# A hybrid decoder layer on one core: the first loads on two queues, the first projection's loop reordered, the planner's clocks and the final norm rewritten

## The chip, the cores and the metric

The kernel runs on one core of a Trainium2 chip. The metric is the device time of one execution in microseconds; lower is better. Three runs of the kernel before the change took 1147.87, 1148.01 and 1148.03 us.

Engine names as in the profile: PE is the matrix engine (PEld its weight loads), DVE the vector engine, ACT the activation engine, POOL the general engine. SP only issues transfers here; "SPq" and "ACTq" are the instruction streams on which a transfer is issued.

## The reference

Input x is 256 tokens by 2048 channels, everything in float32, one layer, then a final norm:

```python
def reference(x, norm1_w, w_in, ..., final_norm_w):
    for l in range(DEPTH):                                  # DEPTH = 1
        h = rmsnorm(x, norm1_w[l])
        x = x + token_mixer(h, w_in[l], ...)                # retention, mLSTM, S5, then w_out
        h = rmsnorm(x, norm2_w[l])
        x = x + conv_ffn(h, ffn_w_up[l], ...)               # 2048 -> 2 x 5632 -> 2048
    return rmsnorm(x, final_norm_w)

def token_mixer(h, w_in, ..., w_out):
    proj = h @ w_in
    r_q, r_k, r_v, r_g, m_qk, m_v, m_o, m_gates, s_u = jnp.split(proj, splits, axis=-1)
    ret_out = jax.nn.silu(r_g) * head_groupnorm(retention(rotary(r_q), rotary(r_k), r_v), ret_gn_w)
    mlstm_out = jax.nn.sigmoid(m_o) * head_groupnorm(mlstm(mq, mk, m_v, i_pre, f_pre), mlstm_gn_w)
    s5_out = s5(s_u, s5_A_re, s5_A_im, s5_log_step, ...)    # diagonal complex scan, gelu, GLU
    return jnp.concatenate([ret_out, mlstm_out, s5_out], axis=-1) @ w_out
```

`rmsnorm` is `x * rsqrt(mean(x*x) + eps) * w`. The S5 part needs, from parameters alone, `exp`, `cos` and `sin` of small tables (128x16 here); the kernel works them out with polynomials on DVE and POOL.

## The kernel before

**Split products.** Every weight chunk (128 rows by up to 1024 columns) is loaded in float32 into a tile `wr` (or `s`, for the first projection's pairs) by one transfer issued at L385. ACT casts it to the high part `wh` (L193), and DVE subtracts to get the low part `wl` (L183). Activations are split the same way: a 512-column tile holds the high part of 256 tokens, then the low part. PE multiplies `wh` with all 512 columns and `wl` with the high 256. The buffers are four `wr`, four `wh` and three `wl`. Nearly all of V's (DVE's) operations are recorded at L183, POOL's at L218, ACT's at L193 or L202 and PE's at L235 (L239 for one transpose helper), because helpers issue them.

**The front.** The first thing to be projected is the S5 input `u`: 16 K tiles of x (128 channels each) against 512 columns of weights `wu`. The loop `for j, ks in enumerate(kts)` runs over ten units: units 0 to 3 are one K tile each (weights 128x512, 256 KB; x 128 KB), units 4 to 9 are two K tiles each (weights 128x1024, 512 KB; x 256 KB). All 20 transfers of x and `wu` are issued by SP, x of a unit just ahead of its weights; the first parameters `pp0` come on ACT's stream. In the loop each unit casts its weights (`highs_to`), splits its x (ACT for the high part with the norm's weight as scale, DVE for the low part), subtracts its low weights (`lows_to`) and then issues eight matmuls for each K tile into four accumulators (`acc, acc, u, u`). `fill(n)` puts n of the small S5 parameter operations (`s5_exps`, 128x16 on DVE) between them; one DVE value of these is the root of a long POOL chain. `square()` squares x for the norm's sum.

**The first norm.** The sum of squares is reduced on PE by matmuls with a matrix of ones (`onesm`), DVE scales it, POOL takes the power -0.5 (`neg_half`) in the midst of its S5 chain, PE transposes that row with `ident` (L239) and the result `rbc` scales the projections.

**The middle, to about 412 us.** The order of all engines is set by a planner. It keeps a modelled clock for each engine (`clk.dve`, `clk.act`, `clk.pe`, `clk.pool`, `clk.dma`); each helper adds a modelled cost in `run()`, and `pump()` steps background generators (retention, gates, mLSTM, S5) when the modelled DVE clock allows. The modelled costs are not times of the chip; they only decide the order. S5's scans, its 128x512 products and the mLSTM's denominators (`t<-mis`, a DVE copy of 128x3 out of PSUM) are such background work.

**The end.** After 412 us a scheduler places the feed-forward part. `last_norm(h)` finishes both token halves: the last two K tiles of the output channels, the sum of squares, the power on POOL, a broadcast by PE (`bc`), the products on DVE, and nine output transfers (L1484, L1491). Each half's group 3 holds 128 columns of `t * r * nft`; for h = 1 it goes out together with channel group 6.

## Time and profile before

| | |
|---|---|
| median of three runs | 1148.01 us |
| profiled execution, its own time | 1147.89 us |
| its span | 1145.8 us |
| PE busy | 1133.7 us, 99% of the span |
| DVE busy | 867.4 us, 76% |
| ACT busy | 626.3 us, 55% |
| POOL busy | 74.8 us, 7% |
| share of the chain that ended last | PE 97%, DVE 2% |
| granted PE clock | 0.998 |
| HBM traffic | 212 MB read, 187 GB/s over the span |

The span runs from the first to the last recorded instruction; the execution's own time is 2.1 us longer. The busy shares are means over parts of different kind: from 100 to 200 us DVE is busy 97.6 us of 100, and from 412 to 1138 us 502.1 of 726. In rows of the timeline the columns are start, duration, engine, line, operation, `out<-in`, shapes, the count of instructions that one row groups, and in brackets the idle time ahead and what ended it.

### The profile page before, as it was taken

Reading aid. Unit: us, or ns where it says so; the run is one execution under the profiler, and the core shown is the slowest. Engines: PE = TensorE matmul, PEld = TensorE weight load, DVE = VectorE, ACT = ScalarE, POOL = GpSimd, SP = SyncE. Lnnn points to the kernel's source line nnn. Section 1 sums busy time; section 2 is a strip of 40 time slices with the busy share of each in tenths; the row PEclk is TensorE's granted clock in tenths of the full one; section 3 lists DMA queues with packets and bytes.
Section 4 is the critical chain, followed back from the end, with each engine's and each line's share of the span. In section 5 each row is a group of like instructions: output and inputs, shape, how many; then the busy total and the mean of one; then the engine's idle time right before and its main releaser. Section 6 shows DMA issues by size and latency. Waiting matters only on the chain.

```text
span 1145.8 us, 18215 instructions
## 1 busy us (share of the span) xinstructions
PE 1133.7 (99%) x6738; PEld 1012.6 (88%) x6738; DVE 867.4 (76%) x1503; ACT 626.3 (55%) x983; POOL 74.8 (7%) x171
## 2 busy tenths in 40 slices
PE   8999999999999999999999999999999999999997
PEld 7899889899988888888888888888888888888897
DVE  8889999799968677777777777777777645444454
ACT  7665557456466555555555555555555444444441
POOL 8406130010000000000000000000000000000000
PEclk9999999999999999999999999999999999999999
DMA  8657545455666655665555565555656566666662
GB/s 316 210 157 244 178 137 162 116 163 159 214 208 216 203 180 190 194 190 188 184 187 194 189 196 186 189 185 188 194 188 199 173 197 176 196 185 193 191 191 107
DMA packets 66905, 215.21 MB, mean 188 GB/s; under 512 B 7552, under 2 KB 9600, under 8 KB 66816
## 3 DMA queue, kind: packets, MB, share of 16 engines
q1 hardware_dynamic: 66672, 214.01, 59.1%
q8 instruction: 52, 0.85, 0.3%
q14 instruction: 37, 0.30, 0.1%
q10 hardware_dynamic: 144, 0.04, 0.0%
HBM read 211.92 MB, written 2.10 MB: 187 GB/s over the span
## 4 chain that ended last, share of the span: by engine, by line
PE 97%; DVE 2%; issue 1%; DMA 0%; ACT 0%; POOLq 0%; POOL 0%; SPq 0%; DVEq 0%
PE acc L235 91%; PE mis L235 3%; DVE s L183 1%; PE wo L235 1%; PE u L235 1%; DVE wl L183 1%; PE mis L239 0%; DMA wr<-in_wu_dram 0%; DVE t L183 0%; DVE tp L183 0%; ACT wh L193 0%; POOLq L1616 0%; POOL t L218 0%; ACT s L202 0%; SPq L1178 0%
## 5 line engine op out<-in xcount | busy, mean ns | idle before, releaser
L193 ACT CAST wh<-wr 128x1024 fp32r<-128x1024 f32 (+3 forms) x409 | 407.8, 998 | 410.5 <-PE acc L235 257.4
L183 DVE TENSOR_TENSOR wl<-wr,wh 128x1024 fp32r<-128x1024 f32 (+3 forms) x409 | 462.7, 1156 | 156.7 <-PE acc L235 105.9
L235 PE MATMUL acc<-s,wh 128*128 128x512 f32 x2372 | 576.0, 392 | 2.8 <-DVE s L183 2.4
L235 PEld LDWEIGHTS acc<-s,wh 128*128 128x128 f32 x2372 | 433.8, 188 | 86.8 <-DVE s L183 3.6
L235 PEld LDWEIGHTS acc<-s,wl 128*128 128x128 f32 x2372 | 308.7, 191 | 14.3 <-issue 0.3
L235 PE MATMUL acc<-s,wl 128*128 128x256 f32 x2372 | 315.3, 283 | 0.0
L235 PE MATMUL acc<-wh,s 128*128 128x384 f32 (+2 forms) x632 | 158.5, 329 | 0.0
L183 DVE TENSOR_TENSOR s<-s,s 128x256 f32<-128x256 f32 (+5 forms) x242 | 111.8, 477 | 46.3 <-ACT s L202 41.5
L183 DVE SCALAR_TENSOR_TENSOR s<-s,pp,s 128x255 f32<-128x255 f32 (+3 forms) x244 | 116.7, 480 | 5.4 <-ACT s L202 2.3
L235 PEld LDWEIGHTS acc<-wh,s 128*128 128x128 f32 x632 | 112.1, 189 | 2.0 <-issue 1.2
L235 PE MATMUL acc<-wl,s 128*128 128x384 f32 (+2 forms) x316 | 103.0, 326 | 0.0
L202 ACT ACTIVATE s<-s,pp 128x256 f32<-128x256 f32 (+1 forms) x146 | 82.4, 569 | 15.2 <-DVE s L183 14.6
L183 DVE TENSOR_TENSOR s<-acc,s 128x256 f32<-128x256 f32 x138 | 57.9, 421 | 41.6 <-ACT s L193 38.0
L202 ACT ACTIVATE s<-s 128x256 f32<-128x256 f32 (+2 forms) x106 | 45.4, 431 | 31.0 <-DVE s L183 30.9
L218 POOL TENSOR_TENSOR t<-t,neg_half 128x2 f32<-128x2 f32 (+1 forms) x4 | 3.4, 858 | 885.6 <-DVE t L183 885.5
L235 PEld LDWEIGHTS acc<-wl,s 128*128 128x128 f32 x316 | 59.7, 189 | 0.1
L193 ACT COPY s<-acc 128x256 f32<-128x256 f32 x136 | 48.6, 359 | 18.0 <-PE acc L235 18.0
L235 PE MATMUL acc<-g,wh 128*128 128x512 f32 x196 | 49.5, 392 | 0.0
L183 DVE TENSOR_TENSOR s<-s,rbc 128x256 f32<-128x256 f32 x106 | 44.5, 424 | 5.7 <-ACT rbc L193 2.7
L235 PEld LDWEIGHTS acc<-g,wh 128*128 128x128 f32 x196 | 35.9, 189 | 6.9
L235 PE MATMUL mis<-s,s 128*32 128x256 f32 (+5 forms) x280 | 29.2, 351 | 0.3 <-DVE t L183 0.3
L235 PEld LDWEIGHTS mis<-s,s 128*32 128x32 f32 (+3 forms) x280 | 21.2, 153 | 5.9 <-issue 1.4
(110 smaller groups left out, 470.1 us busy)
## 6 DMA issues: line engine op xcount, KB each, us to landing
wr<-in_wup_dram SPq DMA_DIRECT2D x176, 512.0 KB, 4.5
wr<-in_wdn_dram SPq DMA_DIRECT2D x70, 512.0 KB, 4.4
wr<-in_wtm_dram SPq DMA_DIRECT2D x56, 384.0 KB, 3.3
wr<-in_wfm_dram SPq DMA_DIRECT2D x36, 512.0 KB, 4.7
wr<-in_wout_dram SPq DMA_DIRECT2D x26, 512.0 KB, 4.7
wr<-in_wdt_dram SPq DMA_DIRECT2D x11, 512.0 KB, 3.6
s<-in_x_dram SPq DMA_DIRECT2D x14, 256.0 KB, 6.2
wr<-in_wdn_dram SPq DMA_DIRECT2D x14, 256.0 KB, 2.7
```

Source lines behind the costliest of these rows:

```text
L183: return real(o, *args, **kw)
L193: return nc.scalar.copy(o, i)
L202: return nc.scalar.activation(o, i, fn, **kw)
L218: return real(o, *args, **kw)
L235: nc.tensor.matmul(o, lhsT=lhsT, rhs=rhs, start=start, stop=stop)
```

## The change

Four things are changed, in the order of the diff.

1. **Clocks of the planner.** The modelled cost of scans, of matmuls of every width, and two start values of clocks are set to other numbers, so the background work of the middle is placed elsewhere.
2. **The first load.** The weights of unit 0 are issued on ACT's stream, ahead of `pp0`, and SP issues x first, then x of unit 1.
3. **The loop.** x's split stands ahead of the unit's weight cast and subtraction (for K tile 0 it is done by DVE), and the small operations are put singly between the others, over more units.
4. **The final norm.** The mean's factor is put in ACT's scale, `t * nft` is formed before the power, the row is broadcast by a transpose in place of a float32 product, ACT scales group 3, which is issued on its own for both halves before the groups 0, 1, 2, and group 3's other half comes last. There are ten output transfers in place of nine.

```diff
--- before.py
+++ after.py
@@ -177,8 +177,8 @@
                     c = 0.07 + 0.00104 * free(args[0])
                 else:
                     c = 0.068 + 0.00104 * n
-                    if fn == "tensor_tensor_scan" and isinstance(args[2], bass.AP):
-                        c += 0.06
+                    if fn == "tensor_tensor_scan":
+                        c += 0.14 + (0.05 if isinstance(args[2], bass.AP) else 0.0)
                 run("dve", c, [o], args + tuple(kw.values()))
                 return real(o, *args, **kw)
             return go
@@ -230,7 +230,7 @@
 
     def mm(o, lhsT, rhs, start, stop, par=1):
         fast = lhsT.dtype == F32R
-        c = max(free(o) / 2400.0, 0.107) * (1 if fast else 4 if free(o) > 64 else 2) / par
+        c = (max(free(o) / 2400.0 + 0.0133, 0.112) if fast else free(o) / 600.0 * (1 if free(o) > 64 else 0.5)) / par
         run("pe", c, [o], [lhsT, rhs])
         nc.tensor.matmul(o, lhsT=lhsT, rhs=rhs, start=start, stop=stop)
 
@@ -382,7 +382,7 @@
             else:
                 t = reuse("wr", wraw.tile([128, CH], F32, tag="wr", name=f"wr{j}"), 4)
             for i, z in enumerate(ap):
-                nc.sync.dma_start(out=t[:, i * n // len(ap):(i + 1) * n // len(ap)], in_=z)
+                (nc.sync if j else nc.scalar).dma_start(out=t[:, i * n // len(ap):(i + 1) * n // len(ap)], in_=z)
             if not auto[0]:
                 free_at = max([x[3] for x in was_read.get(t.tensor.name, ())], default=0.0)
                 clk.dma = max(clk.dma, free_at + 1.3) + n / 703.0
@@ -1155,6 +1155,8 @@
     manual = ctx.enter_context(ExitStack())
     manual.enter_context(tc.manual_schedule())
 
+
+    loads_to(0)
     nc.scalar.dma_start(out=pp0, in_=a["pp"][:, :NP0])
     nc.gpsimd.memset(onesm, 1.0)
 
@@ -1166,7 +1168,7 @@
     warm = mis_t()
     for _ in range(9):
         mm(warm[:, :128], lhsT=onesm, rhs=onesm, start=True, stop=True)
-    clk.pe = 4.8
+    clk.pe = 4.5
 
     xr, xat = [None] * 8, {}
 
@@ -1188,7 +1190,7 @@
     add(ret_heads())
     add(gates())
     add(ml_heads())
-    clk.dve = clk.pool = 3.3
+    clk.dve = clk.pool = 3.7
     add(s5_params(s5_den()))
     add(s5_inputs())
     for c in range(4):
@@ -1236,21 +1238,23 @@
             next(exps, None)
 
     for j, ks in enumerate(kts):
-        fill(3 if j < 2 else 6)
         pump(until=max(last(raw[j].tensor.name), xat[ks[-1]]))
-        if j > 1:
-            highs_to(j)
         for k in ks:
-            d = s2(F32R)
-            S.activation(d[:, :T], xr[k // 2][:, (k % 2) * T:(k % 2 + 1) * T], AF.Copy, scale=P("n1", k))
+            d, x = s2(F32R), xr[k // 2][:, (k % 2) * T:(k % 2 + 1) * T]
+            if k == 0:
+                V.tensor_scalar(d[:, :T], x, P("n1", k), None, op0=MUL)
+            else:
+                S.activation(d[:, :T], x, AF.Copy, scale=P("n1", k))
             xs.append(d)
-        if j > 1:
-            lows_to(j)
+        fill(j == 0)
+
+        n = 2 if 0 < j < NS else 1
         for k in ks:
             V.scalar_tensor_tensor(xs[k][:, T:], xr[k // 2][:, (k % 2) * T:(k % 2 + 1) * T], P("n1", k),
                                    xs[k][:, :T], op0=MUL, op1=SUB)
-        fill(4 if j < 2 else 0)
+            fill(n)
         lows_to(j)
+        fill(n + (j == 0))
         loads_to(j + 4)
         if j + 4 == NU:
             rot = s2()
@@ -1261,6 +1265,7 @@
             st["raws"] = raws
         if j >= NU - 6 and len(sqs) < 8:
             square()
+            fill(1)
         hl = split.pop(j)
         for i, k in enumerate(ks):
             o = [slice(i * 512 + f * 128, i * 512 + (f + 1) * 128) for f in range(4)]
@@ -1465,29 +1470,32 @@
                 mm(pl[h][:, :T], lhsT=x, rhs=z[:, w], start=(k == m == 0), stop=(k == NFF - 1 and m == 2))
 
     def last_norm(h):
-        t, sq, ss, q = s1(), s1(), tn([128, 1]), tn([128, 1])
+        t, sq, ss = s1(), s1(), tn([128, 1])
         V.tensor_tensor(t, pl[h][:, :T], xt[:, h * T:(h + 1) * T], op=ADD)
-        S.activation(sq, t, AF.Square, accum_out=ss)
-        V.tensor_scalar(q, ss, 1.0 / DM, pre[:, h:h + 1], op0=MUL, op1=ADD)
+        S.activation(sq, t, AF.Square, scale=DM ** -0.5, accum_out=ss)
+
+        t3 = s1()
+        V.tensor_tensor(t3, t, nft, op=MUL)
+        q = tn([128, 1])
+        V.tensor_scalar(q, ss, pre[:, h:h + 1], None, op0=ADD)
         r = rsqrt_(q, [128, 1])
         yield
 
         bc = pb[:, h * 128:(h + 1) * 128]
-        mm(bc, lhsT=r.to_broadcast([128, 128]), rhs=ident, start=True, stop=True)
-        for g in (3, 0, 1, 2):
-            if g == 1:
+        tr(bc, r.to_broadcast([128, 128]), ident)
+        o3 = s2()
+        S.activation(o3[:, T:], t3, AF.Copy, scale=r)
+        nc.sync.dma_start(out=out[h, 3][:, T:], in_=o3[:, T:])
+        for n, g in enumerate((0, 1, 2, 3)):
+            if n == 2:
                 yield
-            o = s2()
-            if g == 3:
-                V.scalar_tensor_tensor(o[:, T:], t, r, nft, op0=MUL, op1=MUL)
-                if h == 0:
-                    nc.sync.dma_start(out=out[h, g][:, T:], in_=o[:, T:])
+            o = o3 if g == 3 else s2()
             for c in range(2 * g, min(2 * g + 2, 7)):
                 w = slice((c % 2) * T, (c % 2 + 1) * T)
                 x = xf[c].rearrange("p (k t) -> p k t", k=2)[:, :, h * 128:(h + 1) * 128]
                 V.tensor_tensor(o[:, w].rearrange("p (k t) -> p k t", k=2), x,
                                 bc[:, None, :].to_broadcast([128, 2, 128]), op=MUL)
-            w = slice(0, T if g == 3 and h == 0 else 2 * T)
+            w = slice(0, T if g == 3 else 2 * T)
             nc.sync.dma_start(out=out[h, g][:, w], in_=o[:, w])
 
     for c in range(8):
```

The first place is DVE's instruction order at units 2 to 5 of the front. `wl2` to `wl5` are the low weights, `s2_..<-..,pp0,..` the low parts of x (one for each K tile), and the 128x16 rows the small S5 operations. Before:

```order
L183 TENSOR_TENSOR wl2_226<-wr2_118,wh2_222 128x512
L183 SCALAR_TENSOR_TENSOR s2_39_224<-s2_4_116,pp0_82,s2_39_224 128x256
L183 TENSOR_SCALAR t_38_216<-t_35_213 128x16
L183 TENSOR_SCALAR t_37_215<-t_36_214 128x16
L183 SCALAR_TENSOR_TENSOR t_37_215<-t_37_215,t_36_214 128x16 x4
L183 TENSOR_TENSOR wl3_247<-wr3_121,wh3_243 128x512
L183 SCALAR_TENSOR_TENSOR s2_40_245<-s2_4_116,pp0_82,s2_40_245 128x256
L183 SCALAR_TENSOR_TENSOR t_37_215<-t_37_215,t_36_214 128x16 x2
L183 SCALAR_TENSOR_TENSOR t_24_158<-t_37_215,t_38_216 128x16
L183 TENSOR_TENSOR wl4_267<-s4_6_125,wh4_261 128x1024
L183 SCALAR_TENSOR_TENSOR s2_41_263<-s2_5_123,pp0_82,s2_41_263 128x256
L183 SCALAR_TENSOR_TENSOR s2_42_265<-s2_5_123,pp0_82,s2_42_265 128x256
```

With the change, units 4 and 5:

```order
L183 SCALAR_TENSOR_TENSOR s2_41_248<-s2_5_123,pp0_82,s2_41_248 128x256
L183 TENSOR_SCALAR t_37_235<-t_36_234 128x16
L183 SCALAR_TENSOR_TENSOR s2_42_250<-s2_5_123,pp0_82,s2_42_250 128x256
L183 TENSOR_SCALAR t_37_235<-t_37_235 128x16
L183 TENSOR_TENSOR wl4_258<-s4_6_125,wh4_256 128x1024
L183 SCALAR_TENSOR_TENSOR t_38_236<-t_37_235,t_36_234 128x16
L183 SCALAR_TENSOR_TENSOR t_38_236<-t_37_235,t_38_236 128x16
L183 SCALAR_TENSOR_TENSOR s2_44_280<-s2_7_127,pp0_82,s2_44_280 128x256
L183 TENSOR_SCALAR t_40_238<-t_37_235 128x16
L183 SCALAR_TENSOR_TENSOR s2_45_282<-s2_7_127,pp0_82,s2_45_282 128x256
L183 TENSOR_SCALAR t_39_237<-t_38_236 128x16
L183 TENSOR_TENSOR wl5_290<-s4_8_129,wh5_288 128x1024
```

Before, a unit's low weights come first, then its low x, and no small operation stands behind `wl4`. Now the low x of units 4 and 5 stands ahead of `wl4` and `wl5`, and one small operation stands behind each of these.

The second place is POOL's order around the power of the first norm, `t_111_625<-t_67_490,neg_half_86` before and `t_110_644<-t_67_490,neg_half_86` with the change; the rows around it are the S5 chain. Before:

```order
L218 TENSOR_SCALAR t_98_571<-tp_97_570 128x16 x2
L218 TENSOR_TENSOR tp_99_575<-t_98_571 128x32
L218 TENSOR_SCALAR t_100_576<-tp_99_575 128x16 x2
L218 TENSOR_TENSOR tp_101_580<-t_100_576 128x32
L218 TENSOR_SCALAR t_102_581<-tp_101_580 128x16 x2
L218 TENSOR_TENSOR t_111_625<-t_67_490,neg_half_86 128x2
L218 TENSOR_TENSOR tp_112_629<-t_102_581 128x32
L218 TENSOR_SCALAR t_113_630<-tp_112_629 128x16 x2
L218 TENSOR_TENSOR tp_114_634<-t_113_630 128x32
```

With the change:

```order
L218 TENSOR_TENSOR tp_105_609<-t_89_544 128x32
L218 TENSOR_SCALAR t_106_610<-tp_105_609 128x16 x2
L218 TENSOR_TENSOR tp_107_614<-t_106_610 128x32
L218 TENSOR_SCALAR t_108_615<-tp_107_614 128x16 x2
L218 TENSOR_TENSOR t_110_644<-t_67_490,neg_half_86 128x2
L218 TENSOR_TENSOR tp_111_648<-t_108_615 128x32
L218 TENSOR_SCALAR t_112_649<-tp_111_648 128x16 x2
```

In both the power waits behind a row of chain operations; one stage of the chain (three operations) fewer now stands ahead of it. On PE the matmuls that make its input stand sixteen later than before, and so do the transposes that use it.

The third place is DVE's order around the mLSTM's denominators, `t_30_167<-mis` (before) and `t_22_156<-mis` (after), which PE's next products need. Rows of 128x128 that begin with `t_24_158` or `t_27_163` are S5's scans (the trace calls them TENSOR_TENSOR_SCAN). Before, for the first token half:

```order
L183 TENSOR_TENSOR tp_385_2755<-tp_385_2755,tp_386_2756 128x2 x2
L183 TENSOR_TENSOR wl76_2765<-wr76_2705,wh76_2726 128x768
L183 SCALAR_TENSOR_TENSOR s4_382_2700<-t_24_158,tp_385_2755,s4_381_2699 128x128 x4
L183 TENSOR_TENSOR s4_387_2783<-s4_382_2700,s2_176_1080 128x512 x2
L183 TENSOR_TENSOR s4_388_2784<-s4_382_2700,s2_177_1082 128x512 x2
L183 COPY t_30_167<-mis_383_2742 128x3
L183 COPY t_30_167<-mis_384_2743 128x3
L183 TENSOR_TENSOR wl77_2805<-wr77_2724,wh77_2763 128x768
```

With the change:

```order
L183 TENSOR_TENSOR s4_383_2711<-s4_374_2647,s4_375_2648 128x2x2x128
L183 SCALAR_TENSOR_TENSOR s4_384_2712<-t_27_163,s4_383_2711 128x128 x2
L183 COPY t_22_156<-mis_381_2700 128x3
L183 COPY t_22_156<-mis_382_2701 128x3
L183 SCALAR_TENSOR_TENSOR s4_384_2712<-t_27_163,s4_383_2711 128x128 x2
L183 TENSOR_TENSOR tp_389_2749<-s4_384_2712,t_130_772 128x4
L183 TENSOR_TENSOR tp_390_2750<-s4_384_2712,t_130_772 128x4
L183 TENSOR_TENSOR tp_389_2749<-tp_389_2749,tp_390_2750 128x2 x2
L183 SCALAR_TENSOR_TENSOR s4_384_2712<-t_27_163,tp_389_2749,s4_383_2711 128x128 x2
```

Before, the copies stand behind four scans and four 128x512 products; now behind two scans. For the second token half, before:

```order
L183 SCALAR_TENSOR_TENSOR s4_412_2973<-t_24_158,s4_411_2972 128x128 x2
L183 TENSOR_TENSOR tp_413_2998<-s4_412_2973,t_125_714 128x4
L183 TENSOR_TENSOR tp_414_2999<-s4_412_2973,t_125_714 128x4
L183 TENSOR_TENSOR tp_413_2998<-tp_413_2998,tp_414_2999 128x2 x2
L183 SCALAR_TENSOR_TENSOR s4_412_2973<-t_24_158,tp_413_2998,s4_411_2972 128x128 x4
L183 COPY t_30_167<-mis_409_2961 128x3
L183 COPY t_30_167<-mis_410_2962 128x3
```

With the change:

```order
L183 TENSOR_TENSOR wl79_2857<-wr79_2804,wh79_2832 128x768
L183 TENSOR_TENSOR s2_399_2877<-s2_330_2174,mis_397_2871 128x384
L183 TENSOR_TENSOR wl80_2893<-wr80_2830,wh80_2855 128x768
L183 TENSOR_TENSOR s2_399_2877<-s2_399_2877,mis_398_2872 128x384
L183 TENSOR_TENSOR wl81_2923<-wr81_2853,wh81_2891 128x768
L183 COPY t_22_156<-mis_404_2908 128x3
L183 COPY t_22_156<-mis_405_2909 128x3
L183 SCALAR_TENSOR_TENSOR t_411_2954<-t_22_156 128x12
```

Before, four scans stand right ahead of the copies; now only low weights and one 128x384 product do.

## The prediction

> **What bounds the kernel now.** I read the page's busy times first, then PE's waits, then the timeline where these waits lie.
>
> ```profile
> span 1145.8 us, 18215 instructions
> PE 1133.7 (99%) x6738; PEld 1012.6 (88%) x6738; DVE 867.4 (76%) x1503; ACT 626.3 (55%) x983; POOL 74.8 (7%) x171
> ```
>
> PE idles 12.1 us in all. No edit takes real work from PE (the broadcast at the end aside), so a gain can only come out of this idle time. PE's waits, with the sum, the times and the longest, say where it lies:
>
> ```profile
> PE acc L235 <- DVE s L183: 2.4, 3, 1.5
> PE mis L235 <- POOL t L218: 1.9, 1, 1.9
> PE mis L235 <- DVE t L183: 1.0, 2, 0.8
> PE mis L235 <- POOL onesm L1159: 1.0, 1, 1.0
> PE acc L235 <- ACT wh L193: 0.3, 1, 0.3
> ```
>
> That is 2.7 us in the front (DVE's low x 2.4, a cast 0.3), 1.0 in the middle (the mLSTM's denominators), 1.9 for the last norm's power and 1.0 before the first instruction, which the change doesn't touch. The rest (5.4) comes after the last matmul. So front and middle together can give 3.7, the end some tenths.
>
> **The front.** The timeline at the first pair of K tiles, unit 4:
>
> ```profile
> 4.89 0.73 PE L235 MATMUL acc<-s,wh 128*128 128x512 f32 x2
> ...
> 8.55 0.42 DVE L183 SCALAR_TENSOR_TENSOR t<-t,t 128x16 f32<-128x16 f32 x2
> 8.88 0.71 DVE L183 TENSOR_TENSOR wl<-wr,wh 128x512 fp32r<-128x512 f32 x1
> ...
> 11.55 1.05 ACT L193 CAST wh<-s 128x1024 fp32r<-128x1024 f32 x1 [1.48 <-DMA s<-in_wu_dram]
> ...
> 12.63 1.23 DVE L183 TENSOR_TENSOR wl<-s,wh 128x1024 fp32r<-128x1024 f32 x1
> ...
> 13.77 0.88 DVE L183 SCALAR_TENSOR_TENSOR s<-s,pp,s 128x256 fp32r<-128x256 f32 x2
> ...
> 14.30 0.73 PE L235 MATMUL acc<-s,wh 128*128 128x512 f32 x2 [0.56 <-DVE s L183]
> ...
> 14.89 1.22 DVE L183 TENSOR_TENSOR wl<-s,wh 128x1024 fp32r<-128x1024 f32 x1 [0.25 <-ACT wh L193]
> ...
> 15.33 0.40 PE L235 MATMUL acc<-s,wl 128*128 128x256 f32 x2
> ...
> 16.03 0.87 DVE L183 SCALAR_TENSOR_TENSOR s<-s,pp,s 128x256 fp32r<-128x256 f32 x2
> ...
> 16.83 0.71 DVE L183 TENSOR_TENSOR s<-s,s 128x512 f32<-128x512 f32 x1
> ...
> 17.21 0.62 PE L235 MATMUL acc<-s,wh 128*128 128x512 f32 x2
> ...
> 17.46 1.21 DVE L183 TENSOR_TENSOR wl<-s,wh 128x1024 fp32r<-128x1024 f32 x1
> ```
>
> Unit 4's weights land at 11.55 and are cast by 12.60, yet PE starts at 14.30, because the low x stands on DVE behind `wl4`. With x split first, PE starts behind the cast, at 12.65, if x is there. x is issued ahead of the weights, and with all ahead of it makes 1.88 MB; the weights make that 2.39. By the rates below 2.40 MB have moved at 10.0, and the weights land 1.55 later; 1.88 MB have moved by 8.4, so x lands near 10.0 and its split (0.9 on ACT) is done by 11. PE gains 1.65 at this place. What the units before it lose or win doesn't matter, as long as they end by 12.6: four K tiles at half a pair's 2.91 (14.30 to 17.21) are 5.8, and begin at 4.89, so they could end at 10.7, so 1.9 of waits there is covered, `pp0` behind the first weights included.
>
> When are the weights there? SP's issues of units 3 and 4, and the bytes moved in slices of 1 us from 0:
>
> ```profile
> 4.00 0.43 SPq L385 DMA_DIRECT2D wr<-in_wu_dram  x1
> ...
> 4.95 0.43 SPq L385 DMA_DIRECT2D s<-in_wu_dram  x1
> ```
> ```profile
> GB/s 0 30 275 262 293 301 281 324 289 344 381 404 412 412 414 401 410 393 408 418 406 388 405 399 393 375 213 27 0 29 156 268 283 367 367 299 383 180 188 275
> ```
>
> Two issues lie 0.95 apart, so one transfer fewer on SP brings all behind it 0.47 sooner to the queue. But from 2 us on the bytes flow without a gap, and unit 4 waits 6.6 us from issue to landing: it stands in line behind other bytes. I take its landing as unmoved. The Trainium skill, page "DMA: Bandwidth & Descriptors", section "Issuing engines are not separate DMA queues", says the same from the other side: transfers of all issuing engines run on the same 16 engines and interleave, and a second issuer saves only sequencer time. By the issue rows alone the sum below would be 0.47 lower, by this rule it stays; the GB/s row agrees with the rule.
>
> What is late next is `wl4`, now behind both low x: it runs 12.63 to 13.86 as before, while PE, which needs it 1.03 after its start (14.30 to 15.33), now wants it at 13.68. With 0.1 to hand over it waits 0.28. Behind it DVE's pitches are 1.14 for low weights, 0.80 for two low x, 0.63 for the square's sum and 0.165 for a small operation (8.55 to 8.88 for two). The new order puts four small ones ahead of `wl5`, five and a square sum ahead of `wl6`, three and a sum ahead of `wl7`. The starts follow: 12.63 + 1.14 + 0.80 + 0.66 = 15.23 for `wl5`, done 16.44 and wanted at 16.76 (no wait); 18.46 for `wl6`, done 19.67, wanted 19.56 (0.2); 21.53 for `wl7`, done 22.74, wanted 22.57 (0.27). From there a pair costs DVE 2.57 and PE 2.80, and DVE catches up. The twelve K tiles then take what they took, plus 0.75:
>
> ```profile
> 31.37 2.79 PE acc L235 x16
> ...
> 34.16 1.05 PE mis L235 x8
> 35.22 2.90 PE acc L235 x16
> 38.12 0.22 PE mis L239 x2
> ```
> ```profile
> 14.30:31.37 17.07, 17.07 (x97) 14.99 (x98) 15.55 (x23) 14.36 (x24) 15.60 (x30) 1.00 0.83 304
> ```
>
> 12.65 + 17.07 + 0.75 = 30.47 in place of 31.37: **-0.9**. The row of busy times (PE, PEld, DVE, ACT, POOL) says why not more: DVE is already busy 15.55 us of these 17.07, and gets some ten small operations (1.7) on top. Bounds: without any wait for low weights and with weights 0.47 sooner 12.18 + 17.07 = 29.25, so -2.1; with weights 0.5 later and small operations at 0.2, -0.2. I take the value worked out, since each pitch is measured in the same stage.
>
> **The first norm.** The power stands in POOL's chain, whose root DVE makes:
>
> ```profile
> 7.26 0.60 POOL L218 TENSOR_TENSOR t<-pp,t 128x16 f32<-128x16 f32 x1 [0.20 <-DVE t L183]
> ...
> 14.39 0.33 POOL L218 TENSOR_TENSOR t<-tp,t 128x16 f32<-128x16 f32 x1
> ...
> 15.08 1.12 POOL L218 TENSOR_TENSOR t<-tp,t 128x16 f32<-128x16 f32 x1
> ...
> 36.13 1.64 POOL L218 TENSOR_TENSOR t<-t,neg_half 128x2 f32<-128x2 f32 x1
> ```
>
> The root was ready at 7.06. Spread singly it comes just before `wl3`, near 10.2, so POOL starts 3.0 later; POOL is busy 15.60 of 17.07, so this is not made up. One stage of the chain less ahead (about 0.8) puts the power at 38.3 to 39.95. PE's transposes now stand behind 16 more matmuls (2.90): 30.47 + 2.79 + 2.90 + 1.05 + 2.90 = 40.1. That fits by 0.1. I take **+0.1**; between 0 and +1.5, since one operation of this chain took 0.33 and 1.12 us in neighbouring rounds.
>
> **The middle.** DVE is the busiest engine from 100 to 200 us, and in its order stood, ahead of the two copies that PE waits for:
>
> ```profile
> 210.23 1.61 DVE L183 TENSOR_TENSOR_SCAN s<-t,tp,s 128x128 f32<-128x128 f32 x4
> 211.76 2.47 DVE L183 TENSOR_TENSOR s<-s,s 128x512 f32<-128x512 f32 x4
> ```
> ```profile
> 234.58 1.61 DVE L183 TENSOR_TENSOR_SCAN s<-t,tp,s 128x128 f32<-128x128 f32 x4
> ```
>
> In the new order the first pair stands behind two scans (0.8) in place of four and four products (4.1), the second behind low weights alone. Both waits (0.79 and 0.25, together the 1.0 above) go. But the clocks move all background work up to 412 us, and a row moved away from one place stands somewhere else. The rows of before show no more than two such waits in 380 us; I put half a wait of this kind, 0.3, against it: **-0.7**, between -1.04 (none new) and +0.5 (twice the old ones minus what goes).
>
> **The end.** The power of the second half, and what follows it:
>
> ```profile
> 1139.88 0.48 DVE L183 SCALAR_TENSOR_TENSOR s<-s,t,s 128x256 f32<-128x256 f32 x1 [0.34 <-POOL t L218]
> 1139.89 0.49 PE L235 MATMUL mis<-ident,t 128*128 128x128 f32 x2 [1.94 <-POOL t L218]
> 1140.42 2.41 DVE L183 TENSOR_TENSOR s<-s,mis 128x256 f32<-128x256 f32 x7
> ```
> ```profile
> out_dram<-s SPq DMA_DIRECT2D x7, 256.0 KB, 2.0
> out_dram<-s SPq DMA_DIRECT2D x2, 128.0 KB, 1.7
> ```
>
> The multiply by `nft` adds a product (0.34, 2.41 for seven) on DVE, but beside ACT's square, which the mean waits for; without that cover it would cost 0.34. The broadcast as a transpose costs about 0.2 (the two of L239) in place of 0.49, and the 0.48 on DVE goes to ACT, so the seven products start about 0.2 sooner. They take 0.34 each, and the last transfer lands 0.3 sooner at half the size, if it isn't in line behind the others. The seven products carry 896 KB in 2.41 us, about the rate at which the transfers go, so part of it is lost in line: **-0.3**, between -0.6 and +0.1 (one issue more).
>
> **Sum.** -0.9 + 0.1 - 0.7 - 0.3 = -1.8 against the profiled execution's 1147.89, of which 2.1 lie outside its span. It stands 0.12 below the median of 1148.01, so the forecast is **1146.2 us**.
>
> **Rivals.**
>
> B, the front pays fully: no wait on low weights, weights 0.47 sooner, POOL in time, a clean middle: -2.1 + 0 - 1.04 - 0.3 = -3.4, 1144.6. For it: PE's row shows no wait at all after 14.30 so far. Against it: the GB/s row, and DVE at 91% in the pairs.
>
> C, the change doesn't do what it says: weights land later because two issuers interleave (x of units 0 to 2 now shares with the first weights), small operations cost more among others, the middle gets new waits for the old: -0.2 + 0.1 - 0.2 - 0.1 = -0.4, 1147.6. For it: the data engines are the limit up to 26 us. Against: unit 4 gains 1.65 even with unmoved transfers.
>
> D, slower: POOL's power comes after PE is at the transposes. Nothing on PE passes them, so every microsecond counts. It turns the sum to slower by more than 0.2% when the power is done after 40.1 + 4.1 = 44.2 in place of 39.95: POOL's chain must be 7.3 late, not 3.0; then 1150.3, and more beyond. For it: the chain's operations vary by 0.8, there are some twenty behind the root, and POOL has no idle time to catch up in. Against: its mean is in the 28.9 us measured from root to power already.
>
> **How the numbers follow.** The forecast's case gets 0.56, with its own range 1145.0 to 1147.3; B 0.22, C 0.15, D 0.07. A measurement of this kernel tells 0.2% (2.3 us) from no change, so faster means below 1145.7: 0.9 of B and a third of the forecast's case, 0.38. Slower is above 1150.3: 0.08 with D and what the middle could do beyond its bound. The rest, 0.54, is within. The range, 1144.4 to 1148.2, leaves out D, the lowest part of B and the upper edge of C.
>
> **What would show it.** Right: PE's first matmul of unit 4 close behind its cast, at 12.5 to 12.8; waits of PE on `wl` of 0.2 to 0.3 two or three times, none on low x; the first fm tile near 30.5; no wait on `t<-mis` near 210 and 235; the power done by 40. Wrong: weights of unit 4 landing before 11.2 or after 12; a wait of the transposes on POOL above 1 us; any new wait above 0.5 between 40 and 412 us, or a gap of DVE's low weights there.

## The result and the profile after

The changed kernel takes 1154.2 us (median of four, 1152.9 to 1154.64) against 1147.94 us for the kernel before (four, 1147.67 to 1148.03). The ratio is 1.0052, with a 95% interval of 1.004 to 1.0064: slower by about 6.3 us. The forecast was 1146.2, with a range up to 1148.2, so it was wrong in sign and in size. The profiled execution shown below took 1154.64 us.

The busy times on the page of the changed kernel:

```profile
span 1152.3 us, 18222 instructions
PE 1136.2 (99%) x6736; PEld 1014.0 (88%) x6736; DVE 868.0 (75%) x1504; ACT 626.8 (54%) x984; POOL 86.0 (7%) x171
```

PE has two instructions fewer and is busy 2.5 us more, so some matmuls ran slower. POOL executes the same 171 instructions and is busy 86.0 us where it was 74.8. PE's idle time is 16.1 where it was 12.1. Its waits (sum, times, longest):

```profile
PE mis L239 <- POOL t L218: 5.7, 2, 4.9
PE mis L239 <- DVE s L183: 2.1, 1, 2.1
PE mis L235 <- POOL onesm L1161: 1.0, 1, 1.0
PE acc L235 <- DVE s L183: 0.6, 1, 0.6
PE acc L235 <- ACT wh L193: 0.6, 1, 0.6
PE acc L235 <- DVE t L183: 0.5, 1, 0.5
```

The two copies `t<-mis` are gone, as forecast. The first row is new: two transposes by `ident` wait for POOL, one of them for 4.9 us. (The second row is the broadcast at the end, now a transpose on L239; it stood in the rows of before as a wait for POOL of 1.9.)

The front did what was forecast. The timeline of the changed kernel, from unit 4 to the transposes of the first norm:

```profile
11.49 1.05 ACT L193 CAST wh<-s 128x1024 fp32r<-128x1024 f32 x1 [0.45 <-PE u L235]
...
12.59 0.72 PE L235 MATMUL acc<-s,wh 128*128 128x512 f32 x2 [0.63 <-ACT wh L193]
...
14.99 1.21 DVE L183 TENSOR_TENSOR wl<-s,wh 128x1024 fp32r<-128x1024 f32 x1
...
17.89 1.21 DVE L183 TENSOR_TENSOR wl<-s,wh 128x1024 fp32r<-128x1024 f32 x1
...
20.70 1.23 DVE L183 TENSOR_TENSOR wl<-s,wh 128x1024 fp32r<-128x1024 f32 x1
...
29.87 2.02 PE L235 MATMUL acc<-s,wh 128*128 128x512 f32 x8
...
40.13 0.43 PE L239 MATMUL mis<-ident,t 128*128 128x128 f32 x2 [0.80 <-POOL t L218]
```

Unit 4's matmuls start right behind their cast, at 12.59 in place of 14.30, and the tile that follows the twelve K tiles starts at 29.87 in place of 31.21: 1.34 us gained. At 40.13 the first 0.80 goes back to POOL's power.

The large loss lies at the mLSTM's gates. Their values go through a chain of some fifty operations of 128x12 on POOL, and PE then transposes the result (`ident` against tiles of 128x6). In the kernel before, that place reads:

```profile
86.47 0.89 POOL L218 TENSOR_SCALAR t<-t 128x12 f32<-128x12 f32 x1 [44.48 <-DVE t L183]
...
111.02 1.14 POOL L218 TENSOR_TENSOR t<-tp,t 128x12 f32<-128x12 f32 x1
...
116.07 0.60 PE L239 MATMUL mis<-ident,t 128*6 128x128 f32 x4
```

POOL's last result was there 3.9 us before PE came to it (112.16 to 116.07); such a margin is called slack here. The same place in the changed kernel:

```profile
86.01 7.52 POOL L218 TENSOR_SCALAR t<-t 128x12 f32<-128x12 f32 x1 [39.24 <-DVE t L183]
...
112.86 0.27 PE L239 MATMUL mis<-ident,t 128*6 128x128 f32 x1
...
114.15 3.81 POOL L218 TENSOR_TENSOR t<-tp,t 128x12 f32<-128x12 f32 x1
...
118.01 0.80 PE L239 MATMUL mis<-ident,t 128*6 128x128 f32 x3 [4.88 <-POOL t L218]
...
118.46 3.76 PE L235 MATMUL acc<-s,wh 128*128 128x512 f32 x8
...
122.03 2.35 PE L235 MATMUL acc<-s,wl 128*128 128x256 f32 x16
```

Two things have happened. PE reaches the dependent transposes at 113.13, 2.9 us earlier, since in the new order they stand ahead of 2.8 us of matmuls that stood ahead of them before. (No part does this by itself: with the clocks alone they stand where they stood, with the front alone 2.8 us of matmuls later.) And POOL ends at 117.96, 5.8 us later: its first operation takes 7.52 in place of 0.89, its last 3.81 in place of 1.14 (part of that is made up where POOL waited 2.87 for DVE's reciprocal before, and 0.34 now). A slack of 3.9 has become a stall of 4.88. Behind the stall the matmuls are slow: eight rows of 512 columns run from 118.46 to 122.03, which is 3.57 where a group of eight elsewhere takes 1.84, and the next sixteen take 2.18 to the start of their successor where 1.91 is usual. Together that is another 2.0 us. The table of windows (PE, PEld, DVE, ACT, POOL, then the granted clock) shows why:

```profile
100.00:110.00 10.00, 10.00 (x59) 8.91 (x58) 6.38 (x11) 5.18 (x7) 7.84 (x23) 1.00 0.59 193
110.00:120.00 10.00, 5.12 (x25) 3.96 (x25) 7.89 (x18) 2.21 (x4) 7.29 (x12) 0.79 0.80 252
120.00:130.00 10.00, 10.00 (x55) 8.85 (x54) 9.02 (x17) 6.64 (x10) 0.00 (x0) 0.87 0.37 124
```

The clock granted to PE, as a share of its full speed, falls to 0.79 and 0.87 around the stall and is back at 1.00 from 130 to 140 us. In the row with 0.87 PE is busy throughout, so it is the matmuls themselves that run at the lower clock.

The account from trace to trace, in us of the span (1152.3 - 1145.8 = +6.5): front -1.34; first norm +0.80; two copies in the middle -1.04; the gates' stall +4.88; the clock behind it +2.0; a new wait at 321 us +0.64 (PE for an activation that DVE splits late); the end at most +0.1. That is about 6.0; the other 0.5 was not placed.

### The profile page after: what moved, and what is told of

It reads as the page before. It is cut to its first block, busy times and chain, and to the rows that moved or that the text cites. A ratio compares the mean times of both kernels' runs of the same rounds, so it can differ in the third digit from the quotient of the medians.

```text
span 1152.3 us, 18222 instructions
## 1 busy us (share of the span) xinstructions
PE 1136.2 (99%) x6736; PEld 1014.0 (88%) x6736; DVE 868.0 (75%) x1504; ACT 626.8 (54%) x984; POOL 86.0 (7%) x171
## 4 chain that ended last, share of the span: by engine, by line
PE 71%; DVE 0%; DVEq 0%; issue 0%
PE acc L235 70%; PE wo L235 1%; PE mis L235 1%; DVE s L183 0%; PE mis L239 0%; DVEq L1624 0%; DVE t L183 0%
## 5 line engine op out<-in xcount | busy, mean ns | idle before, releaser
L235 PE MATMUL acc<-s,wh 128*128 128x512 f32 x2372 | 578.5, 393 | 1.8 <-DVE s L183 0.6
L183 DVE TENSOR_TENSOR wl<-wr,wh 128x1024 fp32r<-128x1024 f32 (+3 forms) x409 | 462.2, 1155 | 146.6 <-PE acc L235 97.6
L235 PEld LDWEIGHTS acc<-s,wh 128*128 128x128 f32 x2372 | 434.8, 189 | 86.1 <-DVE s L183 1.6
L235 PEld LDWEIGHTS acc<-s,wl 128*128 128x128 f32 x2372 | 309.0, 191 | 15.1 <-DVE wl L183 0.5
L235 PE MATMUL acc<-s,wl 128*128 128x256 f32 x2372 | 315.5, 283 | 0.1
L235 PE MATMUL acc<-wh,s 128*128 128x384 f32 (+2 forms) x632 | 158.1, 329 | 0.0
L183 DVE TENSOR_TENSOR s<-s,s 128x256 f32<-128x256 f32 (+5 forms) x244 | 112.7, 476 | 46.0 <-ACT s L202 41.5
L183 DVE SCALAR_TENSOR_TENSOR s<-s,pp,s 128x255 f32<-128x255 f32 (+3 forms) x244 | 116.9, 480 | 11.0 <-ACT s L202 7.9
L235 PEld LDWEIGHTS acc<-wh,s 128*128 128x128 f32 x632 | 112.1, 189 | 1.9 <-issue 1.6
L235 PE MATMUL acc<-wl,s 128*128 128x384 f32 (+2 forms) x316 | 103.0, 326 | 0.0
L183 DVE TENSOR_TENSOR s<-acc,s 128x256 f32<-128x256 f32 x138 | 57.8, 420 | 47.0 <-ACT s L193 43.8
L218 POOL TENSOR_TENSOR t<-t,neg_half 128x2 f32<-128x2 f32 (+1 forms) x4 | 2.5, 634 | 899.6 <-DVE t L183 899.6
L235 PEld LDWEIGHTS acc<-wl,s 128*128 128x128 f32 x316 | 59.6, 189 | 0.0
L235 PE MATMUL acc<-g,wh 128*128 128x512 f32 x196 | 49.5, 392 | 0.0
L183 DVE TENSOR_TENSOR s<-s,rbc 128x256 f32<-128x256 f32 x106 | 44.5, 424 | 5.5 <-ACT rbc L193 2.5
L235 PEld LDWEIGHTS acc<-g,wh 128*128 128x128 f32 x196 | 35.8, 188 | 6.9
L235 PE MATMUL mis<-s,s 128*32 128x256 f32 (+5 forms) x280 | 29.2, 351 | 0.0
L235 PEld LDWEIGHTS acc<-g,wl 128*128 128x128 f32 x196 | 25.4, 191 | 1.1
```

The source lines that it names most:

```text
L183: return real(o, *args, **kw)
L218: return real(o, *args, **kw)
L235: nc.tensor.matmul(o, lhsT=lhsT, rhs=rhs, start=start, stop=stop)
```

## The experiments

The **place theory**: the loss comes from where the gates' transposes stand on PE against POOL's chain, and from what that stall does to the clock. Its rivals: one of the four parts is slow by itself (the front's small operations, the second queue, the end); and, within the place theory, POOL's slow operations have a cause of their own.

**The front alone (parts 2 and 3 on the kernel before).**

```diff
-                nc.sync.dma_start(out=t[:, ...], in_=z)
+                (nc.sync if j else nc.scalar).dma_start(out=t[:, ...], in_=z)
...
+    loads_to(0)
...
-        if j > 1:
-            highs_to(j)
...
+            fill(n)
```

> The kernel before with parts 2 and 3 of the change alone (first load on ACT's stream, the loop's order); the planner's clocks and the final norm stay as before. In the order the four gate transposes (identity by t, 128x6) then stand 5.6 us of matmuls later than in the changed kernel. Theory 'place' (the stall of 4.9 us comes from where the transposes stand): they come at about 118.5 us, POOL's chain is done by 118 even if it is as slow as in the changed kernel, so no stall above 0.5 us and no lower clock; front -1.3, norm +0.8 at most, so 1146.5 to 1147.5. Rival 'POOL' (the reordered front and its denser DVE slow POOL's chain wherever it stands): the chain takes 32 us again in place of 25.7, and with a stall of some us the time is 1149 or more.

Measured: 1151.46 against 1148.02, ratio 1.0035 (1.0022 to 1.0048). The gates do not stall, so that half of the theory holds, and POOL's chain takes 24.6 us here (84.96 to 109.56), so the front does not slow it by itself. But the time is missed by 4 us. The front's new order moves the planner's clocks too, and another place breaks: the output projection, in this kernel's timeline and windows:

```profile
311.66 2.35 DVE L183 TENSOR_TENSOR s<-pj,s 128x1024 f32<-128x1024 f32 x2
...
314.45 0.50 PE L235 MATMUL acc<-s,wh 128*128 128x512 f32 x1 [1.26 <-DVE s L183]
...
315.45 0.51 PE L235 MATMUL acc<-s,wh 128*128 128x512 f32 x1 [0.50 <-DVE s L183]
```
```profile
315.00:320.00 5.00, 4.55 (x17) 3.93 (x18) 4.24 (x8) 1.04 (x1) 0.00 (x0) 0.66 0.34 103
```

Two background products of 1.2 us each stand on DVE ahead of the split that PE wants. PE loses 1.26 and 0.50, a third wait of 1.03 follows at 329, and between them the clock is at 0.66 and costs about 1.7; the first norm adds 0.68. Together these are some 5.2; less the front's gain (1.7 here, the next tile starts at 29.49) and the 1.0 of the two copies (their waits are gone here too) that leaves 2.4 of the median's +3.4. The other 1.0 was not placed. (The profiled execution of this kernel took 1153.75, 2.3 over its median, 1.4 of it after the last matmul; that is not explained.)

**The clocks alone (part 1 on the kernel before).**

```diff
+                    if fn == "tensor_tensor_scan":
+                        c += 0.14 + (0.05 if isinstance(args[2], bass.AP) else 0.0)
...
-    clk.pe = 4.8
+    clk.pe = 4.5
...
-    clk.dve = clk.pool = 3.3
+    clk.dve = clk.pool = 3.7
```

> The kernel before with part 1 alone (the planner's costs and start values). The gate transposes stand where they stood before (2.8 us of matmuls later than in the changed kernel). Theory 'place': they come at about 116, POOL's chain is done at 112 to 115; no stall of 4.9. The middle's two waits may go (-1.0) and one of 0.6 near 320 may come: 1147.0 to 1148.2. Rival 'clocks alone are the loss': 1152 or more.

Measured: 1148.63 against 1148.02, ratio 1.0005 (0.9995 to 1.0014), 0.4 above the expected range. Both copies' waits are gone, the gates do not stall, and what is gained there is lost at the first norm, where the power ends at 39.16 in place of 37.77:

```profile
39.21 0.43 PE L239 MATMUL mis<-ident,t 128*128 128x128 f32 x2 [1.33 <-POOL t L218]
```

**The end alone (part 4 on the kernel before).**

```diff
-        mm(bc, lhsT=r.to_broadcast([128, 128]), rhs=ident, start=True, stop=True)
+        tr(bc, r.to_broadcast([128, 128]), ident)
+        o3 = s2()
+        S.activation(o3[:, T:], t3, AF.Copy, scale=r)
```

> The kernel before with part 4 alone (the final norm). From the last weighted matmul to the last instruction the changed kernel takes as long as the kernel before (7.86 against 7.85 us), so 1147.9 within 0.3. By the prediction's term for the end it would be 0.3 faster, 1147.6.

Measured: 1147.72 against 1148.02, ratio 0.9999 (0.999 to 1.0009): nothing that can be told. So the parts alone give +3.4, +0.6 and -0.3, which is 3.7, and together 6.3. They do not add up, because the loss is no cost of a part by itself: parts 1 to 3 move the planner's clocks, and each mixture has its stall at another place.

**The transposes later.** The changed kernel, with only the time at which the planner lets the gates' transposes go to PE set later by 1.0 of its modelled us; they then stand behind 5.6 us more of matmuls.

```diff
-        yield "pe", clk.dve + 0.2
+        yield "pe", clk.dve + 1.2
```

> The changed kernel with one number more: the planner holds the gate transposes back by 1.0 us of its clock, which puts them 5.6 us of matmuls later (behind one more group of 24). Theory 'place': PE comes there at about 118.5, POOL is done at 118.0 at the latest: the stall of 4.88 and the 2.0 us of lower clock behind it go, 1147 to 1148. Rival 'POOL': POOL's chain is what is slow and gets later too, or another wait takes the stall's place: 1150 or more.

Measured: 1149.35, ratio 1.0013 (1.0003 to 1.0022), 1.35 above the expected range. So it stands 1.3 us over the kernel before in place of 6.3. The stall of 4.88 is gone and no low clock is left there, although POOL's first operation is as slow as before:

```profile
85.55 7.52 POOL L218 TENSOR_SCALAR t<-t 128x12 f32<-128x12 f32 x1 [39.24 <-DVE t L183]
```

What remains are the first norm's 0.8 and two new waits that the shift makes:

```profile
PE mis L235 <- DVE s L183: 0.9, 1, 0.9
PE mis L239 <- POOL t L218: 0.8, 1, 0.8
PE mis L235 <- ACT s L193: 0.7, 1, 0.7
```

This shows the place theory for the gates: about 5 of the 6.3 us hang on that one place.

**The front with the old order behind it.** If only the order is to blame, the front with the order of before in everything after the loop should gain. The planner's steps after the loop are written out as a list, taken from the kernel before.

```diff
+        if steps:
+            for n in steps.pop(0):
+                ...
+                step(lst, t)
+            return
```

> The kernel before with parts 2 and 3 (front) alone, and from the end of the front's loop on every step of the planner in exactly the order of the kernel before (the steps are written out as a list of numbers, so the modelled clocks decide nothing). Theory 'place': no gate stall, the gate chain as before (done by about 112.5, wanted at 114.7). But POOL's power of the first norm, with its root 3.0 us later and no operation fewer ahead, is done near 40.9, while PE now wants it at 36.6: a wait of 4 us, and perhaps lower clock behind it; 1150 to 1152.5. Rival: the front's 1.3 us arrive whole because POOL catches up: 1146.7.

Measured: 1152.76 against 1148.21, ratio 1.0039 (1.0023 to 1.0054): slower, as its expectation has it (0.3 above its range), and for another reason than the gates. The old order had the norm's power far back in POOL's chain, and that chain's root now comes 3 us later. Timeline and window (the list adds 21 lines to the kernel's file, so L204, L239, L256 and L260 are here and below what L183, L218, L235 and L239 are above):

```profile
40.43 0.74 POOL L239 TENSOR_TENSOR t<-t,neg_half 128x2 f32<-128x2 f32 x1
...
41.22 0.69 PE L260 MATMUL mis<-ident,t 128*128 128x128 f32 x2 [4.01 <-POOL t L239]
...
41.56 3.38 PE L256 MATMUL acc<-s,wh 128*128 128x512 f32 x8
```
```profile
40.00:45.00 5.00, 3.78 (x12) 3.12 (x13) 2.76 (x8) 0.65 (x2) 4.31 (x17) 0.66 0.35 133
```

The shape is the same as at the gates: a stall of 4.01, and behind it eight matmuls of 3.38 in a window whose clock is 0.66.

**The two prices by themselves.** A small program (the kernel's computation is left out) runs sixteen dependent operations of 128x12 on POOL beside streams of DVE operations, and then blocks of 100 matmuls with gaps of growing length between them.

```diff
+        for i in range(16):
+            nc.gpsimd.tensor_scalar(q, p, 1.0, 0.0, op0=MU, op1=AD)
+        for i in range(count):
+            op()
```

> Leaves out the whole computation of the reference: it measures two costs by themselves. First, sixteen dependent POOL operations of 128x12 beside a stream of DVE: none; subtractions of 128x768 with two inputs in the on-chip memory; products of 128x256 with two; products with one input in PSUM; scalings with one input. Theory 'port': an operation of POOL ends within 0.1 us of the end of a DVE operation when that has two inputs there, and takes 0.2 to 0.3 without; if a stream without gaps can lock POOL out, some operation takes several us (7.5 in the changed kernel). Rival 'cold POOL': the first operation after a pause is slow whatever DVE does. Second, PE streams of 100 matmuls with waits of 0.7 to 5 us between them: theory 'clock': behind a wait above some 1.5 to 2 us the first 8 matmuls of 512 columns take up to 3.6 us in place of 1.84; behind short ones not.

The groups by line and tile (busy us, mean ns of one, idle before); the tile's name tells the stream beside it: `none`, two inputs of 128x768 (`twolong`) or 128x256 (`twoshort`) out of SBUF, one of two inputs out of PSUM (`psum`), one input of 128x1024 (`one`):

```profile
L79 POOL TENSOR_SCALAR qtwolong<-qtwolong 128x12 f32<-128x12 f32 x30 | 27.3, 911 | 2.5
L79 POOL TENSOR_SCALAR qone<-qone 128x12 f32<-128x12 f32 x30 | 19.4, 646 | 2.5
L79 POOL TENSOR_SCALAR qtwoshort<-qtwoshort 128x12 f32<-128x12 f32 x30 | 11.3, 377 | 2.5
L79 POOL TENSOR_SCALAR qnone<-qnone 128x12 f32<-128x12 f32 x30 | 6.0, 199 | 2.5
L79 POOL TENSOR_SCALAR qpsum<-qpsum 128x12 f32<-128x12 f32 x30 | 6.0, 199 | 2.5
```

A POOL operation takes 0.20 alone or beside a stream that reads PSUM, and 0.91 beside long two-input subtractions: it gets in once for each DVE operation. And the gaps (the matmul that follows the gap, with the block it opens):

```profile
244.75 22.98 PE L100 MATMUL pw<-rr,vh 128*128 128x512 f32 x100 [1.66 <-DVE rr L104]
...
269.79 24.59 PE L100 MATMUL pw<-rr,vh 128*128 128x512 f32 x100 [2.06 <-DVE rr L104]
```

After gaps of 0.86, 1.26 and 1.66 the block takes 22.96 to 22.98 in both rounds, and after 0.46 in the second. After 2.06 and 2.66 it takes 24.54 to 24.59, after 3.86 24.57 or 25.85, after 5.66 25.51. So a gap of PE above some bound between 1.66 and 2.06 costs another 1.6 to 2.9 us behind it. While PE rests for 25 us in this program (100 to 125 us), its granted clock reads 0.50; half speed fits the 3.57 us for 1.84 at the gates. The Trainium skill, page "TensorE: Matmul & The Clock Gate", section "HAM oscillation — how this bites in real kernels", has the mechanism, idle time that lowers the clock, with a bound of about 3.4 us; here 2.06 was enough, and the measurement decides.

**A kernel with every order mended.** Parts 2, 3 and 4, the order of the kernel with the clocks alone written out after the loop (it has neither the copies' waits nor the gates' stall), and in it six steps of the S5 chain moved on POOL from ahead of the norm's power to behind it.

> Parts 2, 3 and 4, and behind the front's loop the written-out order of the kernel with the clocks alone (which had no wait between 40 and 412 us), with six steps of POOL's S5 chain moved from ahead of the first norm's power to behind it. Theory 'place': front -1.3, middle -1.0, norm 0 to +0.7, no other wait: 1145.7 to 1146.7. Rival 'POOL or DVE are slower with the new front': waits of 1 us or more in the gates or in the output projection again, 1148 or more.

Measured: 1145.84 against 1148.21, ratio 0.9981 (0.9972 to 0.9989). Its waits on PE:

```profile
PE mis L260 <- DVE s L204: 2.1, 1, 2.1
PE mis L256 <- POOL onesm L1188: 1.0, 1, 1.0
PE acc L256 <- DVE t L204: 0.5, 1, 0.5
PE acc L256 <- ACT wh L214: 0.3, 1, 0.3
```

Between 13.4 and 1137 us PE waits 0.02 in all. So the change's parts do gain what their mechanisms say, 2.4 us, once an order without stalls stands behind them and the norm's power stands further ahead on POOL.

**The same on one queue.** As the last, but the loads issued as before, all by SP.

```diff
-                (nc.sync if j else nc.scalar).dma_start(out=t[:, ...], in_=z)
+                nc.sync.dma_start(out=t[:, ...], in_=z)
...
-    loads_to(0)
```

> The same with the first loads as in the kernel before (weights of unit 0 on SP's stream, the parameters first on ACT's), everything else as in the last. It prices the second queue. By the prediction (landing of unit 4's weights unmoved) it differs by less than 0.3 us; if SP's issues decide, it is 0.5 slower; since the parameters come earlier here, the first matmul could start 0.8 sooner, which is covered until unit 4.

Measured: 1145.66, ratio 0.9978 (0.9969 to 0.9987), on the same chip as the last. The second queue is worth nothing that these runs can tell (0.2 the other way, within the noise). In the two profiles the first matmul comes at 5.65 with it and at 4.83 without, unit 4 starts at 12.03 and 12.33, and the spans are 1143.1 and 1143.5; the medians do not bear that 0.4 out. Both kernels beat the kernel before and the changed one, by about 2.5 and 8.5 us.

**Is POOL slow because it had long been idle?** The changed kernel's order, with five operations of no use on POOL 3.5 us ahead of the gates' chain.

```diff
+            if j == 30:
+                y = tp([128, 12])
+                nc.gpsimd.tensor_scalar(y, l[:, :12].bitcast(F32), 1.0, 0.0, op0=MUL, op1=ADD)
+                for i in range(4):
+                    nc.gpsimd.tensor_scalar(y, y, 1.0, 0.0, op0=MUL, op1=ADD)
```

> The changed kernel in its own order, with five small POOL operations (128x12, used by nothing) that start when the low weights two chunks ahead are written, some 3.5 us ahead of the gates' first operation. Theory 'cold' (that operation took 7.5 us because POOL had rested 39 us): now it takes 0.3 to 0.9, the first of the five may take long instead; the gate chain is done near 112, no stall, 1147.0 to 1147.8. Theory 'DVE' (the run of DVE operations with two on-chip inputs at that place keeps it out): it still takes some us, 1152 or more.

Measured: 1155.9, ratio 1.0058 (1.0039 to 1.0077); one run of the four took 1151.27. The added operations are held up themselves: the first takes 3.26, and of the four right behind it, which find a POOL that has not rested, the first takes 7.70. So the idle time is not the cause. The gates' own first operation, at 95.09, takes 0.42, and their last again 3.81.

```profile
82.54 3.26 POOL L449 TENSOR_SCALAR tp<-wl 128x12 f32<-128x12 f32 x1 [35.67 <-DVE wl L204]
...
85.89 9.23 POOL L451 TENSOR_SCALAR tp<-tp 128x12 f32<-128x12 f32 x4
```

**Is it DVE?** The changed kernel's order, with three small DVE operations that read PSUM put behind the two that make the gates' value. They leave POOL an opening, and cost DVE some 0.5 us.

```diff
+        if t == 1:
+            gap = tn([128, 12])
+            for _ in range(3):
+                V.tensor_scalar(gap, ps[:, 0:12], 1.0, 0.0, op0=MUL, op1=ADD)
```

> The changed kernel in its own order, with three DVE operations more (128x12, from PSUM, used by nothing) behind the two that make the gates' input, where the next in the changed kernel is a subtraction with two on-chip inputs. Theory 'DVE': POOL's first operation gets in beside them and takes under 1 us, the gate chain is done by 112 in place of 118, PE (there at 113.2) waits less than 0.5 and the clock stays: 1147.0 to 1148.0, 6 to 7 us less for 0.4 us more work. Theory 'cold': it takes 7.5 us again, 1154.5.

Measured: 1149.51 against 1148.08, ratio 1.0012 (1.0003 to 1.0022). Its timeline:

```profile
86.18 0.25 POOL L239 TENSOR_SCALAR t<-t 128x12 f32<-128x12 f32 x1 [39.26 <-DVE t L204]
...
111.08 3.81 POOL L239 TENSOR_TENSOR t<-tp,t 128x12 f32<-128x12 f32 x1
...
114.94 0.49 PE L260 MATMUL mis<-ident,t 128*6 128x128 f32 x3 [1.78 <-POOL t L239]
```

The first operation takes 0.25 in place of 7.52, PE's stall falls from 4.88 to 1.78, and no low clock follows a gap of that size: the kernel stands 1.4 us over the kernel before in place of 6.3, for 0.5 us more work on DVE. That DVE's stream holds POOL up is thereby shown. The expected 1147 to 1148 was missed by about what is left: the last operation still takes 3.81. It ends at 114.89, just after DVE's run of operations (114.82, idle behind it). In the changed kernel it is the same: the operation ends at 117.96, DVE's run at 117.89:

```profile
116.68 1.21 DVE L183 TENSOR_TENSOR wl<-wr,wh 128x1024 fp32r<-128x1024 f32 x1
...
119.96 0.48 DVE L183 SCALAR_TENSOR_TENSOR s<-s,pp,s 128x255 f32<-128x255 f32 x1 [2.08 <-ACT s L202]
```

**Which mixture of DVE work does it?** A second small program (computation left out): POOL's chain beside long and short DVE products mixed as in the kernel, plain, with broadcast inputs, dependent on each other, with PE and ACT waiting for them, and all at once.

```diff
+            long(sem)
+            for i in range(4):
+                short(i, sem, bc)
```

> Leaves out the whole computation of the reference: eight dependent POOL operations of 128x12 beside five mixed DVE streams that repeat one subtraction of 128x768 and four products of 128x256, all with two on-chip inputs: plain; with a broadcast second input; with two sums behind that read what the products wrote; with readers on PE and ACT that DVE must signal; all of it together. Theory: POOL gets in once between any two DVE operations, so each of its operations takes at most as long as one DVE operation (0.3 to 1.0 us) in every stream, and the 7.5 us of the changed kernel has another cause. Rival: in one of the mixes an operation of POOL takes 3 us or more; that mix names what keeps it out.

In all five mixtures POOL's first operation, beside a long DVE operation, takes 0.83 to 0.84, and those beside short ones take 0.25; for the plain one:

```profile
7.53 0.84 POOL L79 TENSOR_SCALAR qplain<-dplain 128x12 f32<-128x12 f32 x1 [0.50 <-DVE dplain L75]
...
8.45 2.80 POOL L79 TENSOR_SCALAR qplain<-qplain 128x12 f32<-128x12 f32 x7
```

None holds an operation for 7.5 us. So it stays open what lets some sixteen DVE operations start ahead of one of POOL at 86 us in the changed kernel.

## Why the prediction was wrong

**The step that failed** is in the middle: "a row moved away from one place stands somewhere else ... I put half a wait of this kind, 0.3, against it", with a bound of +0.5. Two things were wrong in it. The price was taken from the waits that happened to exist, both on DVE's copies (0.8 and 0.25), and those waits say nothing of how large the next one may be. What sets it is the slack at the places where PE depends on another engine. At the gates the slack was 3.9 us, it could be read (POOL's last row ends at 112.16, PE's row starts at 116.07), and the new order spent 2.8 of it in one stroke; I compared the order at the two copies only. The rest was spent by POOL, with operations up to 7.52 us where no row of the gates' chain on POOL before was above 2.0 (for three operations). In place of the forecast -0.7 the middle gave +6.5: -1.04 at the copies, +4.88 and +2.0 at the gates, +0.64 at 321 us. A new wait above 0.5 in the middle was the prediction's own sign of being wrong.

**No term had the clock.** A stall was priced at its own length. The runs show 1.6 to 2.9 us on top above a gap of some 2 us, and 2.0 at the gates.

**The front** was right in its mechanism: 12.59 for the forecast 12.65, with the cast at 11.49 (11.55 before). That the weights came no earlier holds for this execution only: in the kernels with the front alone and with the later transposes, whose first loads are the same, the cast starts at 10.25 and 10.28. The term was mis-sized by 0.4, 1.34 for 0.9: the low weights were to cost PE 0.75 and cost 0.37 (from unit 4's first matmul to the next tile 17.28 us, 16.91 before), since a small operation put between large ones on DVE takes about 0.1, not the 0.165 of two in a row; `wl` started at 14.99, 17.89 and 20.70 for the forecast 15.23, 18.46 and 21.53. (Two slips: the forecast 30.47 for the next tile goes by the 31.37 of the chain's view, where the timeline has 31.21; and the 18.46 counts four small operations, as the trace has them, where the sentence says five.)

**The first norm**: the power was done at 40.07 for the forecast 39.95, and PE came at 39.33 in place of 40.1, because the front ended sooner. Hence +0.8 for +0.1, within the bounds given. A gain ahead of a dependence on another engine is partly a loss at it.

**The copies** gave their 1.04. **The end** gave nothing for the -0.3: the product of 0.48 on DVE, which went to ACT, had lain beside PE's broadcast of 0.49, so from the power's end to the seven products it takes 0.50 where it took 0.58. Half the size gave the last transfer nothing either: the four of 128 KB take 2.0 us in the median, where the two before took 1.7 and those of 256 KB take 2.0. From the last matmul to the end it is about 7.9 us in both kernels.

**The rivals.** D, the slower one, named the right kind (PE at a transpose before POOL's result) and the wrong chain; its own case, the first norm, did come when the old order was kept (a stall of 4.01), at a POOL lateness far below the 7.3 that I asked for (the power ends at 41.17, 3.4 later than before), because PE was earlier and the old order had the power further back. The mended order, 1145.7 to 1145.8, has B's conditions on POOL and in the middle, but lies nearer to the forecast's own 1146.2 than to B's 1144.6. C's new waits in the middle came, far larger than its price; its later weights did not.

## What to carry to other kernels

When a change moves work that a planner places, list for every point where the busiest engine depends on another how long the result had been there, and compare each with what the new order takes from it; the waits that a profile shows say nothing about the places that nearly wait. Price a stall with the slow matmuls behind it, and where a stall of PE cannot be avoided keep it under 1.7 us, and no second one close to it. A cheap operation on POOL beside a dense stream of two-input DVE work can take many times its own duration: give it slack, or an opening.

## What was not expected of the hardware

A POOL operation of 128x12 takes 0.20 us alone and 0.91 beside long two-input DVE subtractions (one input of 1024 columns: 0.65; an input out of PSUM: 0.20). The Trainium skill, page "SBUF — State Buffer", section "Who interferes with whom", says that the two engines share a pair of ports under an exclusive lock, and that a DVE operation with two inputs in SBUF contends with a POOL operation that reads SBUF. The 0.91, and the 0.20 beside an input out of PSUM, agree. It does not tell of 7.52 us for one operation, in which some sixteen DVE operations start; with three small DVE operations that read PSUM in DVE's stream it took 0.25, and the small programs did not reproduce it.

In the small program PE slowed after a gap of 2.06 us and not after 1.66; in the kernel a stall of 1.78 was free. In the front-alone kernel two gaps of 1.26 and 0.50 with one matmul between them were enough (0.66 granted), so what counts seems to be idle time in a short stretch rather than one gap; no run separates the two.
